# Reordering the stage between the layer-0 experts and the layer-1 attention

## The chip, the cores and the metric

The kernel runs on one core of one Trainium2 chip. The metric is the device time of one execution in microseconds (us). A profile of one execution, taken by the hardware profiler, is the source of every row below; its times count from the span's start.

## What is computed

Two layers over 512 latent tokens with a prefix of 256 context tokens, 1024 channels, in float32. Layer 0 mixes tokens by pooling, layer 1 by grouped-query attention; each layer ends in 16 experts of which a token uses two. Each sub-layer normalises its input and modulates it with vectors that come from a conditioning vector through `w_mod`:

```python
def modulate(x, g, shift, scale):
    return rmsnorm(x, g) * (1.0 + scale) + shift
...
    qkv = h_lat @ w_qkv
    q = rmsnorm(qkv[..., :Q_DIM].reshape(B, S, N_Q_HEADS, HEAD_DIM), q_g)
    k = rmsnorm(qkv[..., Q_DIM:Q_DIM + KV_DIM].reshape(B, S, N_KV_HEADS, HEAD_DIM), k_g)
    v = qkv[..., Q_DIM + KV_DIM:].reshape(B, S, N_KV_HEADS, HEAD_DIM)
...
    x = x + g1 * y_lat
    x = x + g2 * hier_moe(modulate(x, norm2_g[i], sh2, sc2), ...)
```

The shift of layer 1's first sub-layer is made of chunks 0 and 1 of `w_mod`, its scale of chunks 2 and 3. Latent and context tokens have vectors of their own.

## The kernel before

Tokens are cut into six tiles of 128 rows (two of context, four latent). All instructions stand in an order written by hand; each engine runs its own in that order and waits on semaphores for the others.

**Weights.** The list `order` (lines 267 to 280) fixes the order of all weight loads. Each load is 1 MB, 2048 words in each of 128 partitions. `fill` (line 282) issues the next ones on SP's queue for as long as a place is free and the list has not come to `state["until"]`; `done` gives a place back and fills again, `cap(n)` sets how many of the main places may be filled. Main place i begins at word 48416 - 2048(i + 1): place 0 at 46368, 1 at 44320, 2 at 42272, 3 at 40224, 4 at 38176. Two further places lie in the middle region (`mid`), and two extra ones at words 33728 and 29376, which are used from the middle of attention until the experts of layer 1 (`state["extra"]`, set in `between`). A place is free when no tile lies in it. Tiles come from the class `Arena`: `take` gives the first room that fits, from word 22528 up for plain float32 tiles. A load is issued in the program's order, so one that waits for its place holds up all that SP issues after it.

**Splits.** Products for which float32 is asked for are made of three matmuls on a high and a low part (`mm3`, lines 478 to 481). `split` (lines 473 to 476) makes the parts: ScalarE casts, VectorE or GpSimd subtracts. `split_w` (line 1091) does it for a quarter of a block of `w_qkv`; block 4 holds the keys, block 5 the values, blocks 0 to 3 the queries. The parts of two blocks fit into `w8`, four expert unit buffers of 2048 words.

**Modulation rows.** `mod_row` (line 409) multiplies the conditioning vectors with a chunk of `w_mod` in two halves of eight matmuls (line 415) and splits the result (lines 422, 424). `mod_spread` (line 426) spreads a row over all partitions by a matmul (line 437) and copies it out; for a scale chunk it also multiplies with the norm's gain (lines 434, 442).

**The stage of the change.** The experts of layer 0 call hooks: after expert 13 row 0 is made, after expert 14 row 1, and at the end `last` (line 1117) runs: cap 3, spreads of chunks 0 and 1, splits of the keys, row 2, splits of the values, row 3, spreads of chunks 2 and 3, a square root of a single column, a change of the middle region, and two more unit buffers. Then comes the loop for further blocks (line 874), for experts with more tokens than a tile holds. It uses the last four unit buffers and the count `nb` of blocks; in the profiled execution it has no iteration. Behind it SP loads row tiles 0 to 3 from `accD` (line 1149), into which the experts' results are added by scattering DMAs on GpSimd's queue (line 792). A tile is squared and its root taken on ScalarE (`norm`, lines 457 and 1208), then scaled and shifted on VectorE (`prep`, lines 1214 to 1216), transposed and split (`turn_rows`), and projected on the key and the value weights, twice 24 matmuls. From line 1242 on: norm and prep of tile 0, a fill for the query weights, norm and prep of tile 1, turn_rows of tile 0, norm of tile 2, the load of tile 4, then the loop over six tiles.

**What follows.** The query stage uses four scratch tiles of 2048 words, attention four tiles P of 768 words, four PT of 1536 and the vectors of layer 1. In attention `between` gives the scratch tiles back one by one, lifts the cap to 2, 3 and 4, opens the two extra places, and then works through chunks 4 to 9 of `w_mod`. At the end of attention (from line 1425) the tiles go, the cap is 3, ScalarE's queue loads the four residual row tiles from `accD` (line 1442), the rest of `wo` is split, and `gated` (lines 1453, 1454) adds the first half of the attention's output to the residual before the last two splits.

Of the kernel before, what the change touches and what calls it, by code (L numbers as in the profile page):

```python
# [14 lines left out]
AF = mybir.ActivationFunctionType  # L15
# [5 lines left out]
D = 1024  # L21
S = 512
L = 256
NT = 6
# [4 lines left out]
NE = 16  # L29
# [10 lines left out]

BEFORE = 6
BESIDE = (4, 6)
CAPS = dict(pool=6, moe0=(7,) * 11 + (5,), qkv=3, query=2, attend=(2, 2, 3, 4), wo=3, moe1=(7, 7, 6, 5))


def band_table():
# [179 lines left out]
def backbone(ctx: ExitStack, tc: tile.TileContext, a: dict, out: bass.AP):  # L226
    nc = tc.nc
    V, A, G, T = nc.vector, nc.scalar, nc.gpsimd, nc.tensor
# [15 lines left out]
    def stream_mod(l, chunks):  # L244
        for c in chunks:
            for h in range(2):
                order.append((("mod", l, c, h), a["w_mod"][l, c, h], (4, 512)))
# [5 lines left out]
    def stream_experts(l, between={}):  # L253

        for e in range(-2, NE):
            if e + 2 < NE:
                for h in range(2):
                    order.append((("wgu", l, e + 2, h), a["moe_wgu"][l, nth(e + 2), h], (4, 2 * FE)))
            if e >= 0:
                order.append((("wd", l, e), a["moe_wd"][l, nth(e)], (2, D)))  # L260
            for m, c in between.get(e, ()):
                stream_mod(m, [c])

    def stream_qkv(c):
        order.append((("qkv", c), a["attn_wqkv"][c], (8, 256)))
# [2 lines left out]
    order.append((("pool",), a["pool_w"], (8, 256)))  # L268
    stream_mod(0, range(6, 10))
    stream_experts(0, {-2: [(0, 10), (0, 11)], 12: [(1, 0)], 13: [(1, 1)]})  # L270
    stream_qkv(4)
    stream_qkv(5)
    stream_mod(1, range(2, 4))
    for c in range(4):
        stream_qkv(c)
    stream_mod(1, range(4, 10))
# [641 lines left out]
    m0 = Moe(0, NT)  # L918
# [172 lines left out]
    def split_w(c, q, eng=V):  # L1091

        i = (4 * c + q) % 8
        u = shaped(w8[:, 1024 * i:1024 * i + 1024], [128, 2, 2, 256])
        split(u[:, 0], u[:, 1], get("qkv", c)[:, 2 * q:2 * q + 2, :], eng)
        if q == 3:
            done("qkv", c)
        return u
# [4 lines left out]
    wkv = {}  # L1103

    def mod1_row(*chunks):
        for c in chunks:
            for _ in mod_row(1, c, mod1[c]):
                pass
# [3 lines left out]
    def spread1(*chunks):  # L1112
        for c in chunks:
            for _ in mod_spread(sm, 1, c // 2, c % 2, mod1[c], {v: bc["BA"[c // 2], v] for v in range(2)}):
                pass

    def last():

        state["until"] = ("qkv", 0)
        cap(CAPS["qkv"])  # L1120
        pb.split(t=(2, 1), y=(2, 1), m=(4, 1))
        bc.update({(n, v): sx.tile([128, D]) for n in ("B", "A") for v in range(2)})
        spread1(0, 1)
        wkv[4] = [split_w(4, q) for q in range(4)]
        mod1_row(2)
        wkv[5] = [split_w(5, q) for q in range(4)]
        mod1_row(3)
        spread1(2, 3)

        A.activation(m0.sb.tile([128, 1]), eps, AF.Sqrt)  # L1130
        pb.split(t=(2, 1), u=(2, 1), y=(2, 1), i=(1, 1), m=(1, 1))
        ar.swap("mid")
        for _ in range(2):
            m0.more_units()

    m0.experts(accD, CAPS["moe0"], more, {
        11: tables, 12: lambda: state.update(mid=0), 13: lambda: mod1_row(0), 14: lambda: mod1_row(1), NE: last})
    m0.sb.free()
    m0.mb.free()


    ab = ar.scope()
    vv = ab.tile([128, NT, 256])
    xb = [sx.tile([128, D]) for t in range(4)]
    x = [xb[t % 4] for t in range(NT)]
    sx.reserve(2, [128, D], "h1")

    def load_rows(t):
# [48 lines left out]
        V.tensor_sub(c[:, :, 1, :], q, c[:, :, 0, :])  # L1197

    sk = ar.scope()
    wK, wV = wkv[4], wkv[5]  # L1200
    r = sk.tile([128, NT])
    ks = sk.tile([128, NT, 4])
    pb.split(t=(4, 1), k=(2, 1), v=(2, 1))
# [1 line left out]
    def norm(t):  # L1205
        if t < NT:
            square_sum(sk, x[t], r[:, t:t + 1])
            A.activation(r[:, t:t + 1], r[:, t:t + 1], AF.Sqrt, scale=1.0 / D, bias=eps)

    def prep(t):  # L1210
        if t < NT:
            v = 1 if t < 2 else 0
            h1[t] = sx.tile([128, D], name="h1", bufs=2)
            V.tensor_mul(h1[t], x[t], bc["A", v])
            V.reciprocal(r[:, t:t + 1], r[:, t:t + 1])
            V.scalar_tensor_tensor(h1[t], h1[t], r[:, t:t + 1], bc["B", v], op0=OP.mult, op1=OP.add)  # L1216
# [18 lines left out]
    def store_key(t):  # L1235
        for kv in range(0, 4, 2):
# [2 lines left out]
                T.transpose(p2[:, j, :], kc[t][:, kv + j // 2, j % 2].rearrange("p a d -> p (a d)"), ident)  # L1239
            A.copy(kT[:, kv:kv + 2, :, t * 128:t * 128 + 128], p2.rearrange("p (a b) c -> p a b c", a=2))  # L1240

    norm(0)
    prep(0)
    state["until"] = None
    fill()
    norm(1)
    prep(1)
    turn_rows(0)
    norm(2)
    load_rows(4)  # L1250
    for t in range(NT):
        PK[t] = pb.get("k", [128, 256])
        project(PK[t], t, wK)
        if t:
            key(t - 1)
            A.copy(vv[:, t - 1, :], PV[t - 1])
        if t + 1 < NT:
            turn_rows(t + 1)
            if t + 5 < NT:
                load_rows(t + 5)  # L1260
        square_heads(sk, PK[t], ks[:, t, :])
        A.activation(ks[:, t, :], ks[:, t, :], AF.Sqrt, scale=1.0 / HEAD, bias=eps)
        norm(t + 3)
        prep(t + 2)
        PV[t] = pb.get("v", [128, 256])
        project(PV[t], t, wV)
        if t:
            store_key(t - 1)
    wq = {0: [split_w(0, q) for q in range(4)]}
# [272 lines left out]
```

## Time and profile before

| what | us |
|---|---|
| three runs | 931.96, 924.33, 931.01 |
| their median | 931.01 |
| the profiled execution | 926.72 |
| its span, first to last instruction | 924.9 |

In the rows PE is TensorE (PEld its weight loads), DVE VectorE, ACT ScalarE, POOL GpSimd, SP the engine that issues most loads; ACTq and SPq are their queues. L415 is line 415. A timeline row gives the start, the time, the engine, line and operation, output and input tile, their shape and the count; in brackets stands how long the engine had been idle and what ended it. PEclk is TensorE's granted clock, 1.00 for 2.4 GHz and 0.50 for 1.2 GHz.

### The profile page before, as it was taken

The numbers are of one execution on the slowest core, as the hardware profiler recorded it, in microseconds if no ns is written. First come the engines' busy times: TensorE is split into PE (matmuls) and PEld (weight loads), VectorE is DVE, ScalarE is ACT, GpSimd is POOL, SyncE is SP. The second block draws the span as 40 slices with busy tenths as digits, with TensorE's granted clock in tenths as the row PEclk, the third lists the DMA queues.
The fourth block names the chain that finished last, engine by engine and source line by source line (L and its number), as shares of the span: only waits on it lengthen the run. The fifth ranks groups of instructions, "written<-read, shape, count | busy, mean of one in ns | idle before, by whom it ended". The sixth has DMA issues, their size and how long they took to land. (4 is left out here: it accounts for less than half of the span.)

```text
span 924.9 us, 12774 instructions
## 1 busy us (share of the span) xinstructions
PE 802.5 (87%) x4593; PEld 541.8 (59%) x4593; DVE 614.0 (66%) x1077; ACT 481.9 (52%) x1006; POOL 172.8 (19%) x164
## 2 busy tenths in 40 slices
PE   4699958989999865998879999999979599999994
PEld 0256735567766514987766566566657355666551
DVE  3552778799998545746666677768245678888761
ACT  2534346446555335755568677679323364555440
POOL 1052332223333210003200000002200212332211
PEclk9899977999999975999999999999998789999997
DMA  8997369989998966011101332310074599999961
GB/s 339 418 349 311 128 217 413 348 300 357 377 362 304 356 217 273 2 47 46 46 1 46 139 135 92 109 74 27 20 311 196 203 364 309 343 335 330 344 239 29
DMA packets 36722, 204.80 MB, mean 221 GB/s; under 512 B 6660, under 2 KB 6740, under 8 KB 16816
## 3 DMA queue, kind: packets, MB, share of 16 engines
q1 hardware_dynamic: 24976, 172.06, 48.5%
q0 software_dynamic: 10032, 27.30, 11.3%
q10 hardware_dynamic: 1648, 4.60, 1.3%
q8 instruction: 37, 0.61, 0.3%
q14 instruction: 29, 0.24, 0.1%
HBM read 187.15 MB, written 25.17 MB: 230 GB/s over the span
## 5 line engine op out<-in xcount | busy, mean ns | idle before, releaser
L479 PE MATMUL banks<-low 128*128 128x512 f32 (+2 forms) x404 | 154.6, 383 | 6.1 <-DVE main L1191 4.4
L480 PE MATMUL banks<-low 128*128 128x512 f32 (+2 forms) x404 | 150.3, 372 | 7.4 <-DVE low L476 7.4
L481 PE MATMUL banks<-low 128*128 128x512 f32 (+2 forms) x404 | 150.3, 372 | 0.0
L476 DVE TENSOR_TENSOR low<-main,low 128x1024 fp32r<-128x1024 f32 (+1 forms) x121 | 129.8, 1129 | 22.4 <-ACT low L475 22.0
L475 ACT CAST low<-main 128x1024 fp32r<-128x1024 f32 (+1 forms) x137 | 119.3, 933 | 5.9 <-DMA main<-in_moe_wgu_dram 2.8
L1380 DVE TENSOR_REDUCE main<-banks 128x1 f32<-128x768 f32 x64 | 61.1, 955 | 43.7 <-PE banks L1376 43.3
L479 PEld LDWEIGHTS banks<-low 128*128 128x128 f32 (+1 forms) x404 | 74.6, 185 | 24.4 <-ACT low L475 6.9
L480 PEld LDWEIGHTS banks<-low 128*128 128x128 f32 (+1 forms) x404 | 74.6, 185 | 22.4 <-DVE low L476 8.0
L481 PEld LDWEIGHTS banks<-low 128*128 128x128 f32 (+1 forms) x404 | 74.5, 184 | 17.3 <-DVE low L476 0.8
L790 PE MATMUL banks<-main 128*128 128x512 f32 (+1 forms) x176 | 81.1, 604 | 2.4 <-SPq L874 1.5
L415 PE MATMUL banks<-main,cT 128*32 128x512 f32 x376 | 61.4, 756 | 14.3 <-DMA main<-in_w_mod_dram 12.4
L476 POOL TENSOR_TENSOR low<-main,low 128x512 fp32r<-128x512 f32 x16 | 20.7, 1296 | 282.2 <-ACT low L475 282.2
L1398 ACT COPY main<-banks 128x384 f32<-128x384 f32 x128 | 56.0, 487 | 33.5 <-PE banks L1397 33.1
L1401 ACT ACTIVATE main<-banks,main 128x768 f32<-128x768 f32 x64 | 63.7, 996 | 8.4 <-DVE main L1384 3.5
L742 POOL DMA_INDIRECT main<-hD,main x32 | 42.1, 1317 | 118.5 <-issue 39.6
L776 ACT COPY main<-banks 128x256 f32<-128x256 f32 (+1 forms) x32 | 11.1, 346 | 100.2 <-PE banks L774 92.7
L791 DVE TENSOR_TENSOR main<-banks,main 128x512 f32<-128x512 f32 (+1 forms) x64 | 43.0, 687 | 30.5 <-PE banks L790 28.9
L470 PE MATMUL banks<-ident,main 128*128 128x128 f32 (+2 forms) x384 | 49.7, 273 | 13.8 <-DVE main L1216 9.3
L1397 PE MATMUL banks<-ident,main 128*128 128x128 f32 x384 | 54.1, 274 | 4.3 <-ACT mid L1285 2.0
L1409 PE MATMUL banks<-main 128*64 128x256 f32 x384 | 53.8, 394 | 2.0 <-DVE low L1387 2.0
L470 PEld LDWEIGHTS banks<-ident,main 128*128 128x128 f32 (+2 forms) x384 | 42.0, 145 | 20.5 <-DVE main L1216 10.0
L790 PEld LDWEIGHTS banks<-main 128*128 128x128 f32 (+1 forms) x176 | 30.4, 181 | 37.5 <-issue 32.3
(258 smaller groups left out, 1471.5 us busy)
## 6 DMA issues: line engine op xcount, KB each, us to landing
main<-in_moe_wgu_dram SPq DMA_DIRECT2D x50, 1024.0 KB
main<-in_w_mod_dram SPq DMA_DIRECT2D x47, 1024.0 KB
main<-in_moe_wd_dram SPq DMA_DIRECT2D x22, 1024.0 KB
mid<-in_moe_wgu_dram SPq DMA_DIRECT2D x14, 1024.0 KB
mid<-in_moe_wd_dram SPq DMA_DIRECT2D x10, 1024.0 KB
main<-in_attn_wqkv_dram SPq DMA_DIRECT2D x6, 1024.0 KB
hD<-main POOLq DMA_DIRECT2D x9, 512.0 KB, 3.3
main<-in_attn_wo_dram SPq DMA_DIRECT2D x4, 1024.0 KB
```

Of the source, the lines that this page charges most:

```text
L415: T.matmul(p[32 * j:32 * j + 32, :], cT[:, 4 * h + j, :], w[:, j, :], start=h == 0, stop=h == 1)
L470: T.transpose(p[:, k, :], src[:, c * 128:c * 128 + 128], ident[:n, :n])
L475: A.copy(hi, src)
L476: eng.tensor_sub(lo, src, hi.bitcast(F32))
L479: T.matmul(p, xh, wh, start=first, stop=False)
L480: T.matmul(p, xh, wl, start=False, stop=False)
L481: T.matmul(p, xl, wh, start=False, stop=last)
L790: T.matmul(p, hT[:, k, :], wd[:, k, cols], start=k == 0, stop=k == 1)
L1380: V.reduce_max(m[:, 0:1], p, axis=AX.X)
L1397: T.transpose(p2[:, j, :], Ps[u][:, k * 128:k * 128 + 128], ident)
L1398: A.copy(PT[u // 4, hh][:, 3 * g3:3 * g3 + 3, 128 * q2:128 * q2 + 128], p2)
L1401: A.activation(Ps[step], p, AF.Exp, bias=mx[step][:, 0:1], scale=rq, accum_out=mx[step][:, 1:2])
```

## The change

Chunks 2 and 3 of layer 1's `w_mod` are loaded ahead of the key and value weights. The hook at the end of the experts makes row 2, spreads chunks 0 and 1, makes row 3, spreads chunks 2 and 3, and splits the keys, all ahead of the loop; the cap of the stage is 2. The stop at the first query block is set from expert 13 on. The two further unit buffers go, and the middle region changes behind the loop. The value weights are split behind prep of tile 1. The single square root stands behind the loop. turn_rows of tile 0 comes ahead of norm and prep of tile 1, and the fill for the query weights behind the value splits. Two tiles, `gap`, of 1024 words are taken and never used.

```diff
@@ -40,7 +40,7 @@
 
 BEFORE = 6
 BESIDE = (4, 6)
-CAPS = dict(pool=6, moe0=(7,) * 11 + (5,), qkv=3, query=2, attend=(2, 2, 3, 4), wo=3, moe1=(7, 7, 6, 5))
+CAPS = dict(pool=6, moe0=(7,) * 11 + (5,), qkv=2, query=2, attend=(2, 2, 3, 4), wo=3, moe1=(7, 7, 6, 5))
 
 
 def band_table():
@@ -268,9 +268,9 @@
     order.append((("pool",), a["pool_w"], (8, 256)))
     stream_mod(0, range(6, 10))
     stream_experts(0, {-2: [(0, 10), (0, 11)], 12: [(1, 0)], 13: [(1, 1)]})
+    stream_mod(1, range(2, 4))
     stream_qkv(4)
     stream_qkv(5)
-    stream_mod(1, range(2, 4))
     for c in range(4):
         stream_qkv(c)
     stream_mod(1, range(4, 10))
@@ -1114,35 +1114,34 @@
             for _ in mod_spread(sm, 1, c // 2, c % 2, mod1[c], {v: bc["BA"[c // 2], v] for v in range(2)}):
                 pass
 
+    def hold():
+        mod1_row(0)
+        state["until"] = ("qkv", 0)
+
     def last():
 
-        state["until"] = ("qkv", 0)
         cap(CAPS["qkv"])
         pb.split(t=(2, 1), y=(2, 1), m=(4, 1))
         bc.update({(n, v): sx.tile([128, D]) for n in ("B", "A") for v in range(2)})
+        mod1_row(2)
         spread1(0, 1)
-        wkv[4] = [split_w(4, q) for q in range(4)]
-        mod1_row(2)
-        wkv[5] = [split_w(5, q) for q in range(4)]
         mod1_row(3)
         spread1(2, 3)
-
-        A.activation(m0.sb.tile([128, 1]), eps, AF.Sqrt)
+        wkv[4] = [split_w(4, q) for q in range(4)]
         pb.split(t=(2, 1), u=(2, 1), y=(2, 1), i=(1, 1), m=(1, 1))
-        ar.swap("mid")
-        for _ in range(2):
-            m0.more_units()
 
     m0.experts(accD, CAPS["moe0"], more, {
-        11: tables, 12: lambda: state.update(mid=0), 13: lambda: mod1_row(0), 14: lambda: mod1_row(1), NE: last})
+        11: tables, 12: lambda: state.update(mid=0), 13: hold, 14: lambda: mod1_row(1), NE: last})
     m0.sb.free()
     m0.mb.free()
+    ar.swap("mid")
 
 
     ab = ar.scope()
     vv = ab.tile([128, NT, 256])
     xb = [sx.tile([128, D]) for t in range(4)]
     x = [xb[t % 4] for t in range(NT)]
+    gap = [sx.tile([128, D]) for t in range(2)]
     sx.reserve(2, [128, D], "h1")
 
     def load_rows(t):
@@ -1197,7 +1196,6 @@
         V.tensor_sub(c[:, :, 1, :], q, c[:, :, 0, :])
 
     sk = ar.scope()
-    wK, wV = wkv[4], wkv[5]
     r = sk.tile([128, NT])
     ks = sk.tile([128, NT, 4])
     pb.split(t=(4, 1), k=(2, 1), v=(2, 1))
@@ -1239,18 +1237,21 @@
                 T.transpose(p2[:, j, :], kc[t][:, kv + j // 2, j % 2].rearrange("p a d -> p (a d)"), ident)
             A.copy(kT[:, kv:kv + 2, :, t * 128:t * 128 + 128], p2.rearrange("p (a b) c -> p a b c", a=2))
 
+
+    A.activation(r[:, NT - 1:NT], eps, AF.Sqrt)
     norm(0)
     prep(0)
+    turn_rows(0)
+    norm(1)
+    prep(1)
+    wkv[5] = [split_w(5, q) for q in range(4)]
     state["until"] = None
     fill()
-    norm(1)
-    prep(1)
-    turn_rows(0)
     norm(2)
     load_rows(4)
     for t in range(NT):
         PK[t] = pb.get("k", [128, 256])
-        project(PK[t], t, wK)
+        project(PK[t], t, wkv[4])
         if t:
             key(t - 1)
             A.copy(vv[:, t - 1, :], PV[t - 1])
@@ -1263,7 +1264,7 @@
         norm(t + 3)
         prep(t + 2)
         PV[t] = pb.get("v", [128, 256])
-        project(PV[t], t, wV)
+        project(PV[t], t, wkv[5])
         if t:
             store_key(t - 1)
     wq = {0: [split_w(0, q) for q in range(4)]}
```

## Rows read from the trace of the kernel before

**Rows 1.** The page: busy time, then tenths in 40 slices of the span.

```profile
PE 802.5 (87%) x4593; PEld 541.8 (59%) x4593; DVE 614.0 (66%) x1077; ACT 481.9 (52%) x1006; POOL 172.8 (19%) x164
...
DMA  8997369989998966011101332310074599999961
```

**Rows 2.** Timeline of TensorE, 330 to 363: start us, us, engine, line.

```profile
331.30 1.07 PE L415 MATMUL banks<-main,cT 128*32 128x512 f32 x8
...
335.47 1.93 PE L415 MATMUL banks<-main,cT 128*32 128x512 f32 x8 [3.10 <-DMA main<-in_w_mod_dram]
...
340.53 1.94 PE L415 MATMUL banks<-main,cT 128*32 128x512 f32 x8 [2.40 <-DMA main<-in_w_mod_dram]
...
343.85 1.93 PE L415 MATMUL banks<-main,cT 128*32 128x512 f32 x8 [1.39 <-DMA main<-in_w_mod_dram]
...
359.21 1.97 PE L470 MATMUL banks<-ident,main 128*128 128x128 f32 x8 [9.26 <-DVE main L1216]
...
362.34 0.58 PE L481 MATMUL banks<-low,mid 128*128 128x256 f32 x1 [0.54 <-DVE mid L476]
```

**Rows 3.** Windows from 330 on: length, busy us (instructions), PEclk, DMA share, GB/s.

```profile
340.00:345.00 5.00, 3.09 (x16) 0.43 (x16) 1.94 (x4) 0.82 (x2) 0.00 (x0) 0.50 0.27 98
...
360.00:365.00 5.00, 4.46 (x20) 3.94 (x19) 2.85 (x5) 2.51 (x5) 0.00 (x0) 0.50 1.01 424
...
375.00:380.00 5.00, 5.00 (x45) 5.00 (x44) 4.25 (x9) 4.44 (x15) 0.00 (x0) 1.00 0.01 2
```

**Rows 4.** End of attention: timeline of SP, ScalarE, VectorE, TensorE; one of the waits.

```profile
674.92 0.80 SPq L295 DMA_DIRECT2D main<-in_moe_wgu_dram  x2
...
674.94 1.97 ACTq L1442 DMA_DIRECT2D main<-accD  x4
...
DVE main L1454 <- DMA main<-accD: 6.2, 3, 2.3
...
693.83 1.29 DVE L476 TENSOR_TENSOR low<-main,low 128x512 fp32r<-128x512 f32 x2
...
694.57 0.80 PE L480 MATMUL banks<-low 128*128 128x512 f32 x1 [7.04 <-DVE low L476]
...
696.54 0.77 PE L479 MATMUL banks<-low 128*128 128x512 f32 x1
...
700.54 0.40 PE L480 MATMUL banks<-low 128*128 128x512 f32 x1
```

**Rows 5.** Timeline of SP's DMA issues, 312 to 353; us ends with the last.

```profile
312.45 1.57 SPq L295 DMA_DIRECT2D main<-in_attn_wqkv_dram  x2
...
315.77 20.14 SPq L295 DMA_DIRECT2D main<-in_w_mod_dram  x4
...
325.27 4.71 SPq L295 DMA_DIRECT2D main<-in_w_mod_dram  x2
...
351.61 1.77 SPq L1149 DMA_DIRECT2D main<-accD  x4
```

**Rows 6.** Timeline of ScalarE and VectorE, 332 to 377.

```profile
332.38 2.19 ACT L475 CAST low<-main 128x512 fp32r<-128x512 f32 x4
...
333.05 2.50 DVE L476 TENSOR_TENSOR low<-main,low 128x512 fp32r<-128x512 f32 x4 [2.70 <-ACT low L475]
...
354.88 1.06 ACT L457 ACTIVATE main<-main 128x1024 bf16<-128x1024 f32 x1 [0.89 <-DMA main<-accD]
...
356.05 1.28 ACT L1208 ACT_TABLE_LOAD   x1
...
357.35 0.29 ACT L1208 ACTIVATE main<-main,eps 128x1 f32<-128x1 f32 x1
...
376.29 1.04 ACT L457 ACTIVATE main<-main 128x1024 bf16<-128x1024 f32 x1
```

**Rows 7.** Waits of SP, 330 to 362: us in total, times, longest us.

```profile
SPq L874 <- DVEq L873: 7.4, 1, 7.4
SPq L874 <- DMA accD<-main: 5.4, 2, 4.9
```


## The prediction

> **What bounds the kernel now.** I read the page's busy table and slices first: TensorE is busy 87% of the span and the DMA engines are full in both expert stages but nearly empty in the attention between them [rows 1]. So a change can only pay where TensorE stands still, and there are two such places that the change can reach. The windows and the timeline show the first: after the experts of layer 0 TensorE waits for the modulation rows (chunk 2's second half starts at 335.47, chunk 3's halves at 340.53 and 343.85, each after a wait for in_w_mod), then from about 350 until 359.21 it does nothing, 9.26 us, waiting for VectorE's first normalised tile [rows 2]. In that time the DMA engines run dry: share 0.27 in 340:345 [rows 3]. TensorE comes back at 0.50 of its clock (1.2 GHz) and runs 20 matmuls in 4.46 us where it later, at 1.00, runs 45 in 5.00 [rows 3]. The second place is the end of attention: TensorE waits 7.04 us at 694.57 for a split that VectorE makes late, because VectorE waited 6.2 us for the residual rows out of accD [rows 4]. Those rows were asked for at 674.94, the same moment at which SP asks for the first two expert weights of layer 1 [rows 4].
>
> **Part 1: the order of the six loads.** At one freed place each, SP issues now: key and value weights at 312.45 and 313.70, chunk 2's halves at 315.77 and 325.27, chunk 3's at 329.66 and 335.58 [rows 5]. The last waits for the key splits, whose first pass ends at 333.05 + 2.50 = 335.55 [rows 6]. Putting chunks 2 and 3 in front leaves the moments that places come free as they are, so the loads by name become: chunk 2 at 312.45 and 313.70, chunk 3 at 315.77 and 325.27, key weights at 329.66. With the cap at 2 the value weights take place 0, which chunk 2's first half leaves about 330.1 (its eight matmuls can start when the last down projection ends near 329.6, and take 1.07 us, the row at 331.30 [rows 2]). I give each load the landing of the load that has its issue time now: the first three are in by 331.30, the fourth at 335.47, the fifth at 340.53 [rows 2]. Value weights, 5.5 us earlier than the sixth load now, land by 343.85 at the latest.
> From chunk 3's second half to SP's release take now 351.61 - 343.85 = 7.76 us [rows 2, 5]; from 335.47 that gives 343.2. The key splits now come behind the spreads and ahead of the loop: 3.17 us from first cast to last subtraction (332.38 to 335.55 [rows 6]), so 340.53 + 3.17 = 343.70, and SP issues some 0.4 later, 344.1. A third arrival is the scatter of the last expert: SP's two long waits at the loop are 4.9 us for accD and then 7.4 us for VectorE, the latter ending just before 351.61 [rows 7], so the scatters land at about 344.0. All three agree; I take 344.4 for the row loads against 351.61: **7.2 us**. Bounds: the value load now competes with the last scatter, and 1 MB at 424 GB/s [rows 3] is 2.5 us, so 4.7 at worst; 8.4 if only the spreads hold SP (343.2).
>
> **Part 2: the loop and the square-root table.** The loop for further blocks now uses the last four of six unit buffers; two of them lie under the value splits, which is why these go behind the loop. The loop runs no iteration here, so the buffers cost nothing, and moving the change of the middle region behind it costs at most a wait for weights read long ago: 0. The warm-up activation ahead of the loop goes, and one comes behind it. In the trace the first one is in vain: the square at 354.88 is followed by a table load of 1.28 us at 356.05 before the root at 357.35 [rows 6], on the chain to the first tile. With a root issued behind the loop, its load lies in the 3.27 us from 351.61 to 354.88 in which the rows travel [rows 5, 6]; no square after 357.35 reloads. Saved: **1.3 us**; bounds 0 (the square still wants its own set) and 1.3.
> The Trainium skill, ScalarE: Activation LUTs, What ACT_TABLE_LOAD costs, puts a switch of set at some 1.28 us of load and 1.38 us of drain, 2.66 in all. The row has 0.02 us between the load's end and the root, so I see no drain; by the page the saving would be 2.7 and the time 1.4 us less.
>
> **Part 3: order of tiles and value splits.** turn_rows(0) moves ahead of the second tile's norm. Today VectorE finishes prep(1) before the first subtraction, and the third matmul of the projection waits 0.54 us [rows 2]; now the subtraction is next in line: **0.5 us**. The value splits, 2.50 us of VectorE like the key's [rows 6], stand behind prep(1). By the offsets of the trace the first tile's product ends at 350.6, subtractions 353.9, prep(1) 356.5, value splits 359.0. TensorE's first projection of 24 matmuls at half clock (4.46/20 each [rows 3]) lasts until about 357.3, eight transposes go to 358.1, and the first value projection needs the third quarter of the splits (358.4) only at its 13th matmul: hidden. If that cover is gone, the cost is at most the 2.5 us.
> A wait is added on SP: the fill for the query weights wants place 0, held until the value splits end at 359.0; behind it stand the second query block and row tiles 4 and 5. Two blocks and a half-megabyte tile at 424 GB/s, 2 us after issue, bring tile 4 at about 367. Its square is at 376.29 now [rows 6], about 367.2 then; ScalarE may wait a fraction of a us, and TensorE needs that tile only three projections later: 0, at worst 1. Two places instead of three mean that query blocks 2 and 3 are asked for when blocks 0 and 1 are split, four projections of 24 x 0.111 us = 10.7 us [rows 3] ahead of use, with the queue idle: 0.
> First place in all: 7.2 + 1.3 + 0.5 = **9.0 us**.
>
> **Part 4: where the tiles come to lie.** The two gap tiles hold no data. They push the two h1 tiles from 29312 to 31360 and the small key tiles behind 33408. When the query stage asks for room, first fit then gives its scratch 2 the words 29376 to 31424 (now it misses by 64 words, since the key tiles begin at 31360, and goes to 33728) and scratch 3 goes to 33728 instead of 35776. In attention the four P tiles then lie at 22824 and 31424 to 33728 (now 22824 and 29376 to 31680) and the PT tiles at 35776 to 41920 (now up to 42432). So place 2 (42272 to 44320) and the extra place at 29376, both covered now, are free: five places in attention instead of three. The stream then runs two loads further: the last modulation half leaves a place for the first expert load, and the first wo block for the second, all in a stage with idle queues [rows 1]. At 674.9 nothing is left for SP to issue until the next wo block is split at about 678. The residual rows, four of 0.5 MB, have the queues alone: 2.1 MB at 424 GB/s [rows 3] are 5 us, and with one modulation load beside the tail they are in by 685, while VectorE adds the fourth at 687. Its 6.2 us of waits go. The split that TensorE waits for comes at 688.3 instead of 694.5; TensorE then stands 0.7 us, and 0.5 more for the first product's transposes, not 7.04. It also keeps its clock: from 696.54 to 700.54 it runs 11 steps of 512 columns in 4.00 us [rows 4]; at 1.00 a 256-column one takes 5.00/45 = 0.111 us [rows 3], so I estimate 0.22 for these, 2.4 us in all, and with the same ratio on the two steps and the transposes from 694.57 to 696.54 some 2.3 us come back. Sum 7.04 - 1.2 + 2.3 = **8.1 us**. Bounds: 0 if the places do not come free, 9.3 if TensorE does not stand at all. In the expert stage of layer 1 TensorE is dense and the bytes still to load are the same, so the gain is carried to the end.
>
> **Sum.** 926.72 (span 924.9 and 1.8 around it) - 9.0 - 8.1 = 909.6. The profiled execution is 4.3 us below the median of the runs, 931.01, so the forecast for a median is 931.0 - 17.1 = **914**.
>
> **Rivals.** (a) Only the first place gains: something I have not placed still covers place 2 or 29376, or the rows come late for another reason. 931.0 - 9.0 = 922. For it: the argument is by words of memory, no row shows it. Against: both extra addresses fit the scratch tiles exactly. (b) Only the second gains, because the scatters or the value load hold the loop until 351 anyway: 931.0 - 8.1 = 923. For it: the accD wait ends only near 344, and the value load is 1 MB more in the queue; against: the DMA share is already down at 0.27 in 340:345 now [rows 3]. (c) The change does not do what it says, both at nothing: 931. (d) Slower: TensorE's clock does not come back in the key and value stage, because value splits on ScalarE and VectorE open gaps between its matmuls. The stage has 12 projections of 24 matmuls; at 0.50 a matmul costs 0.223 instead of 0.111 us [rows 3]. Now some 20 run slow [rows 3]; beyond about 150 more slow ones (17.1/0.112) the gain is used up, and with all 268 the loss is 30.0 and the time 944. Against: the clock rises now in spite of the 0.54 us gap, and my offsets leave no larger one.
>
> **How the numbers follow.** About 1%, 9.3 us, is what a measurement of this kernel can tell from no change (three runs lie 7.6 apart). Forecast 0.68, with its own range 907 to 920; (a) 0.14; (b) 0.08; (c) 0.05; (d) 0.05. Faster by over 1% (under 921.7): nearly all of the forecast and half of (a) and (b), which sit on the bound: 0.75. Slower: (d) and a little of the rest, 0.07. Same: 0.18. The range 903 to 926 takes in the forecast, (a) and (b).
>
> **What would show it.** Right: row loads by SP at 344 to 345; no table load between the first square and its root; TensorE's first transposes at about 350.7 (359.21 now); two layer-1 expert loads issued before the end of attention; no wait for accD at the residual add, and TensorE's 7 us gap under 2. Wrong: the accD or in-flight wait at the loop ending after 348; a first value projection with gaps; expert loads still issued with the residual rows.

## The result and the profile after

The changed kernel took 914.93 us (median of four runs, 913.24 to 916.75), the kernel before 929.53 beside it: ratio 0.9863, 95% interval 0.9824 to 0.9902, so 12.7 us saved, between 9.1 and 16.4. This ratio, like all that follow, is an estimate with its interval and not the quotient of the two medians, which lie 14.6 apart. Forecast was 914.0, a gain of 17.1. The profiled execution took 913.42 with a span of 911.6.

From the page of the changed kernel [rows 1]:

```profile
PE 800.0 (88%) x4593; PEld 540.1 (59%) x4593; DVE 613.8 (67%) x1077; ACT 479.4 (53%) x1004; POOL 173.1 (19%) x164
...
DMA  8979268989999993311210542220155699999962
```

The work is the same (TensorE has as many instructions, VectorE too, ScalarE two fewer). What went is idle time. Two loads have moved forward in the DMA row: slices 27 and 29 read 2 and 1 where they read 1 and 0, and slice 30, in which attention ends, reads 5 where it read 7 (the slices of the two pages do not cover quite the same stage).

TensorE behind layer 0's experts [rows 2], start, length, engine, line, and in brackets the idle time with what ended it:

```profile
339.47 1.06 PE L415 MATMUL banks<-main,cT 128*32 128x512 f32 x8 [0.61 <-DMA main<-in_w_mod_dram]
...
354.63 1.97 PE L470 MATMUL banks<-ident,main 128*128 128x128 f32 x8 [11.05 <-DVE main L1214]
...
357.14 0.58 PE L481 MATMUL banks<-low,mid 128*128 128x256 f32 x1
```

Here a shift has to be taken out first. Layer 0's last down product ends at 329.62 in the trace of before and at 333.63 in this one. The 4.01 us arise almost wholly in the first 105 us, in code that is the same in both. So from here on times of the first place are counted from that end, called zero. The transposes come 21.00 us behind zero, against 29.59. The wait of 0.54 at the third matmul of the projection is gone.

SP's issues in the timeline [rows 5], the second fence its waits at the loop [rows 7] (us in total, times, longest):

```profile
333.66 1.35 SPq L295 DMA_DIRECT2D main<-in_attn_wqkv_dram  x2
348.35 1.77 SPq L1148 DMA_DIRECT2D main<-accD  x4
```

```profile
SPq L874 <- DMA accD<-main: 10.0, 2, 5.0
...
SPq L874 <- DMA main<-in_attn_wqkv_dram: 0.5, 1, 0.5
SPq L874 <- DVEq L873: 0.4, 1, 0.4
```

The row loads leave 14.72 behind zero; predicted was 344.4, which is 14.8 behind. The last three waits follow one another: the puts (the scattering DMAs into `accD`), VectorE at the last of the key splits (0.4 more), the value weights (0.5 more). VectorE's timeline ahead of the loop:

```profile
344.29 1.29 DVE L442 SCALAR_TENSOR_TENSOR main<-banks,main 128x512 f32<-128x512 f32 x2 [0.73 <-ACT main L434]
345.50 2.49 DVE L476 TENSOR_TENSOR low<-main,low 128x512 fp32r<-128x512 f32 x4
```

The last spreads (line 442) and then the key splits (line 476) follow one another without a gap, and the splits end at 347.99, 0.36 ahead of the row loads. VectorE held SP for 7.4 before.

ScalarE's timeline on the way to the first tile [rows 6]:

```profile
348.35 1.28 ACT L1241 ACT_TABLE_LOAD   x1 [1.71 <-DVEq L874]
349.65 0.20 ACT L1241 ACTIVATE main<-eps 128x1 f32<-128x1 f32 x1
351.58 1.06 ACT L457 ACTIVATE main<-main 128x1024 bf16<-128x1024 f32 x1 [1.73 <-DMA main<-accD]
...
352.76 0.29 ACT L1206 ACTIVATE main<-main,eps 128x1 f32<-128x1 f32 x1
```

The table is loaded while the rows travel; between square and root nothing is left.

The end of attention in the timeline [rows 4], SP, ScalarE's queue and TensorE:

```profile
596.12 44.51 SPq L295 DMA_DIRECT2D main<-in_moe_wgu_dram  x2
...
670.76 1.79 ACTq L1443 DMA_DIRECT2D main<-accD  x4
...
684.10 0.50 PE L480 MATMUL banks<-low 128*128 128x512 f32 x1 [0.75 <-DVE low L476]
...
685.30 0.65 PE L470 MATMUL banks<-ident,main 128*128 128x128 f32 x4 [0.47 <-DVE main L522]
...
688.11 0.39 PE L480 MATMUL banks<-low 128*128 128x512 f32 x1
```

Layer 1's first two expert loads leave SP at 596.12 and 640.30, long before the residual rows at 670.76. VectorE no longer waits for accD there, and TensorE's stop of 7.04 is 0.75 and 0.47. From the last output cast of attention (ScalarE, 0.06 before the rows are asked for) to the first routing matmul it takes 46.95 instead of 55.68, and to the end of the span 240.90 instead of 250.02.

### The profile page after: what moved, and what is told of

It reads as the page before. It is cut to its first block, busy times and chain, and to the rows that moved or that the text cites. A ratio compares the mean times of both kernels' runs of the same rounds, so it can differ in the third digit from the quotient of the medians.

```text
span 911.6 us, 12768 instructions
## 1 busy us (share of the span) xinstructions
PE 800.0 (88%) x4593; PEld 540.1 (59%) x4593; DVE 613.8 (67%) x1077; ACT 479.4 (53%) x1004; POOL 173.1 (19%) x164
## 5 line engine op out<-in xcount | busy, mean ns | idle before, releaser
L479 PE MATMUL banks<-low 128*128 128x512 f32 (+2 forms) x404 | 153.0, 379 | 5.9 <-DVE main L1190 4.4
L480 PE MATMUL banks<-low 128*128 128x512 f32 (+2 forms) x404 | 148.2, 367 | 1.1 <-DVE low L476 1.1
L481 PE MATMUL banks<-low 128*128 128x512 f32 (+2 forms) x404 | 148.5, 368 | 0.0
L479 PEld LDWEIGHTS banks<-low 128*128 128x128 f32 (+1 forms) x404 | 73.2, 181 | 23.9 <-ACT low L475 6.7
L481 PEld LDWEIGHTS banks<-low 128*128 128x128 f32 (+1 forms) x404 | 72.9, 180 | 17.1 <-DVE low L476 0.8
L480 PEld LDWEIGHTS banks<-low 128*128 128x128 f32 (+1 forms) x404 | 73.3, 182 | 15.9 <-DVE low L476 1.7
L470 PEld LDWEIGHTS banks<-ident,main 128*128 128x128 f32 (+2 forms) x384 | 41.8, 145 | 22.2 <-DVE main L1214 11.4
```

Of the source, the lines that this page charges most:

```text
L470: T.transpose(p[:, k, :], src[:, c * 128:c * 128 + 128], ident[:n, :n])
L479: T.matmul(p, xh, wh, start=first, stop=False)
L480: T.matmul(p, xh, wl, start=False, stop=False)
L481: T.matmul(p, xl, wh, start=False, stop=last)
```

## The experiments

The table has each profiled execution's stages: from zero to the row loads, to the first transposes and to the last output cast, then from that cast to the routing matmul and to the end of the span. The kernels are those of the experiments below; each row is one execution.

| kernel | rows | transposes | cast | to routing | to end |
|---|---|---|---|---|---|
| before | 21.99 | 29.59 | 345.26 | 55.68 | 250.02 |
| changed | 14.72 | 21.00 | 337.07 | 46.95 | 240.90 |
| no gap tiles | 14.99 | 21.34 | 337.33 | 55.73 | 249.26 |
| gap tiles alone | 21.96 | 29.64 | 345.36 | 47.10 | 244.81 |
| hold by order | 18.00 | 24.37 | 338.87 | 46.96 | 239.71 |
| values ahead | 19.09 | 25.50 | 341.52 | 46.94 | 240.28 |
| order alone | 18.43 | 26.10 | 341.24 | 55.85 | 249.00 |
| root in the chain | 15.91 | 23.56 | 338.18 | 46.97 | 239.67 |
| keys behind | 12.45 | 19.23 | 333.85 | 46.94 | 241.25 |
| loads behind the cast | 14.11 | 20.42 | 334.60 | 51.43 | 245.82 |
| keys halved | 12.78 | 19.09 | 333.66 | 47.12 | 240.33 |
| loads with the rows | 13.91 | 20.17 | 334.83 | 55.88 | 247.86 |
| turn behind | 17.31 | 23.59 | 340.46 | 47.41 | 239.60 |
| changed, again | 15.02 | 21.38 | 335.76 | 46.99 | 240.16 |

**The two places apart.** First the changed kernel without the gap tiles, then the kernel before with nothing but them.

```diff
-    gap = [sx.tile([128, D]) for t in range(2)]
```

> The changed kernel without the two gap tiles. By the theory of places, the words 29376 to 31424 and place 2 are covered again in attention, so the two expert loads are issued at the end of attention with the residual rows, TensorE's stall there is 7 us again, and the stage from the cast of the last attention output to the end of the span lasts 250 us (as before), not 241. The stage from the end of the last down product to the first transposes stays at 21.0 us. Time 8 to 9 us above the changed kernel, 923. Rival (the end of attention gained by its phase or clock, not by places): no difference, 915.

> The kernel before with the two gap tiles added and nothing else. By the theory of places: two expert loads are issued before the end of attention, the stall falls from 7.0 to 0.7 us, the stage from the cast of the last attention output to the end of the span lasts 241 us, the stage ahead of the first transposes stays at 29.6 us; 921 against 929.5. Rival: no difference.

Without the gap tiles: 917.94, ratio 0.9898 (0.9862 to 0.9934), 9.5 us saved. With them alone: 920.92, ratio 0.9931 (0.9904 to 0.9958), 6.4 saved. The sum is 15.9, and the table shows that each part moves its own stage and leaves the other as it was. The time without the gap tiles is better than the 923 that was expected: the last stage loses its 8.4 us as forecast (249.26 against 240.90), but the time is 3.0 above the changed kernel's 914.93 and 5.8 above the 912.19 of the next kernel, which is the changed one in effect. Without the gap tiles VectorE waits for the rows again (a row of its waits), and TensorE stands as before at the end of attention (its timeline):

```profile
DVE main L1454 <- DMA main<-accD: 6.2, 3, 2.3
```

```profile
686.43 0.80 PE L480 MATMUL banks<-low 128*128 128x512 f32 x1 [6.95 <-DVE low L476]
```

With them alone the stop is 0.91 (TensorE's timeline) and routing comes 8.6 us sooner behind the cast:

```profile
687.65 0.50 PE L480 MATMUL banks<-low 128*128 128x512 f32 x1 [0.91 <-DVE low L476]
```

But 3.8 of it are lost between routing and the end (197.71 us against the changed kernel's 193.95), where TensorE has a wait that it has not in the changed kernel. From its timeline:

```profile
751.20 1.51 PE L470 MATMUL banks<-ident,main 96*128 96x96 f32 x8 [3.21 <-DMA main<-hD,main]
```

Whether that kernel always has it stays open. What both runs show is that rivals (a) and (b), one part without the other, each fell.

**Holding the expert loads back, first try.** The changed kernel, with the queue's list stopped ahead of layer 1's experts until attention is over.

```diff
         state["extra"] = 2
+        state["until"] = ("wgu", 1, 0, 0)
         fill()
...
+    state["until"] = None
     cap(CAPS["wo"])
```

> The changed kernel, places free as they are, but the stream stops ahead of the first expert load until the end of attention, as it does in the kernel before for want of places. If it is the two expert loads beside the residual rows that cost the time (contention in the DMA queues), the 7 us stall and the half clock behind it come back and the time is 8 us above the changed kernel, 923. Rival (the earlier modulation loads, or other data in other words, bring the gain): 915.

The edit did nothing to the times of issue. It only moved the issues down in the program, and SP, which has nothing else to do there, ran ahead to them (its timeline):

```profile
594.96 42.97 SPq L295 DMA_DIRECT2D main<-in_moe_wgu_dram  x2
```

Neither theory is tested by it. It is the changed kernel a second time: 912.19, ratio 0.9837 (0.979 to 0.9884), 15.1 us saved. But its row loads leave at 18.00 behind zero, not 14.72, and this is of use. SP waits 4.0 for VectorE at the loop, and the cause lies further back, in the landing of chunk 3's second half (TensorE's timeline):

```profile
337.86 1.11 PE L415 MATMUL banks<-main,cT 128*32 128x512 f32 x8 [3.50 <-DMA main<-in_w_mod_dram]
```

That is 8.74 behind zero (329.12) where the changed kernel has 5.84 (339.47 - 333.63). From there to the row loads it is 9.26 here and 8.88 there, the spreads and the key splits. Why that half lands later stays open.

**The value splits ahead of the loop.**

```diff
         wkv[4] = [split_w(4, q) for q in range(4)]
+        wkv[5] = [split_w(5, q) for q in range(4)]
...
-    wkv[5] = [split_w(5, q) for q in range(4)]
```

(With the region change and two buffers as the kernel before has them there.)

> The changed kernel with the value splits ahead of the loop again, and with the two further unit buffers that they then need. If putting them behind the loop matters, SP is released only when the value load has landed (14.1 us behind the last down product in the changed kernel) and its splits are done, 3.2 us later: row loads at 17.7 instead of 14.7 us, first transposes at 24 instead of 21.0; 918. Rival (the order of the loads is all): 21, 915.

TensorE's timeline, then VectorE's:

```profile
337.59 1.07 PE L415 MATMUL banks<-main,cT 128*32 128x512 f32 x8 [2.46 <-DMA main<-in_w_mod_dram]
```

```profile
343.73 4.90 DVE L476 TENSOR_TENSOR low<-main,low 128x512 fp32r<-128x512 f32 x8
```

Eight subtractions instead of four. From the modulation half's matmuls to the row loads it is 11.4 us (348.99 - 337.59), 2.1 more than the 9.26 above. So putting the value splits behind the loop is worth some 2 us, where 3 was expected. The time, 913.76 (ratio 0.9856, 0.9806 to 0.9907), does not resolve that.

**The order alone.** The kernel before, with the modulation halves first in the list and the spreads ahead of both splits.

```diff
+    stream_mod(1, range(2, 4))
     stream_qkv(4)
     stream_qkv(5)
-    stream_mod(1, range(2, 4))
...
+        spread1(0, 1)
...
         spread1(2, 3)
+        wkv[4] = [split_w(4, q) for q in range(4)]
+        wkv[5] = [split_w(5, q) for q in range(4)]
```

> The kernel before with only the load order (all four row halves ahead of the key and value weights) and the order of rows, spreads and splits changed; both splits stay ahead of the loop, the places stay as they were. Counted from the end of layer 0's last down product. Theory (the modulation rows' last load ends last ahead of the loop): spreads end some 12 us in when that load is in time, 8 vector subtractions of both splits (4.9) follow, row loads 17 to 19 us in against 22.0 before, first transposes 24 to 26 in against 29.6, the end of attention as before (TensorE stall near 7, routing matmul 55.7 behind the last cast): 3 to 5 us faster, 923 to 925. Rival (the loop's entry hangs on the last put or the value weights, and the order gives nothing): row loads 21 to 22 in, 928.

925.59, ratio 0.9982 (0.996 to 1.0004): 1.7 us, and hardly to be told from nothing. In the stages it is 3.5 to the transposes and 4.0 to the cast, as expected. Chunk 3's half lands 7.03 behind zero, and the row loads leave 11.4 later, as with the values ahead. The order moves the modulation rows out of the chain, but both splits take their place: by itself it is worth half of the 8.2 that the changed kernel gains up to the cast.

**The root.** The changed kernel without the lone root behind the loop.

```diff
-    A.activation(r[:, NT - 1:NT], eps, AF.Sqrt)
```

> The changed kernel without the lone square root behind the loop, so that the table is loaded at the first norm's root. Theory: the load (1.28) stands between the first square and its root, first transposes 7.6 us behind the row loads' issue instead of 6.3, and 1.3 us more in all, not readable in one time. Rival (the table load lies beside the vector product, and the chain does not lengthen): 6.3 and no change.

ScalarE's timeline:

```profile
348.48 1.06 ACT L457 ACTIVATE main<-main 128x1024 bf16<-128x1024 f32 x1 [5.04 <-DMA main<-accD]
...
349.64 1.28 ACT L1206 ACT_TABLE_LOAD   x1
350.94 0.29 ACT L1206 ACTIVATE main<-main,eps 128x1 f32<-128x1 f32 x1
```

From row loads to transposes 7.65 us, against 6.28 and 6.36 in the two profiles of the changed kernel, and 7.60 before. The load's 1.28 is all that is added there. The one time, 908.90, says nothing about so small a piece.

**The key splits behind the loop.** SP's waits say that they end last, so they were moved into the time in which the rows travel, and the value weights held behind the row loads.

```diff
-        state["until"] = ("qkv", 0)
+        state["until"] = ("qkv", 5)
...
-        wkv[4] = [split_w(4, q) for q in range(4)]
...
     for t in range(4):
         load_rows(t)
+    state["until"] = ("qkv", 0)
+    fill()
+    wkv[4] = [split_w(4, q) for q in range(4)]
```

> The changed kernel with the key splits moved directly behind the loop (they lie in the wait for the rows) and the value weights' load held until the row loads are issued. Theory (three arrivals end the wait at the loop, the key splits the last of them by a little, more when the last modulation load is late): the wait now ends with the last put, some 13.6 us behind the last down product, or with the spreads, 12 to 15 in; row loads 14 us in when the modulation load is in time and up to 16 when late, against 14.7 and 18.0 to 19; first transposes 6.3 to 6.6 behind them; 0.5 to 2.4 us faster than the changed kernel: 911.5 to 913.5, ratio to before near 0.983. Rival (the value weights' transfer beside the rows delays the second rows, or the splits hold the first square and the first projection): 1 to 2 us slower, 915 to 917.

The one wait that SP has left at the loop, and VectorE and ScalarE in the timeline:

```profile
SPq L874 <- DMA accD<-main: 9.3, 2, 6.2
```

```profile
342.57 1.23 DVE L1214 TENSOR_TENSOR main<-main 128x1024 f32<-128x1024 f32 x1
...
343.10 1.04 ACT L457 ACTIVATE main<-main 128x1024 bf16<-128x1024 f32 x1
```

Only the puts are left to wait for, and the row loads leave 12.45 behind zero (14 was expected, with the puts ending the wait later). Half a us of it goes again, because ScalarE, with four casts and the table load, starts the square 0.53 late. 910.37, ratio 0.9832 (0.9796 to 0.9869), with runs from 903.78 to 915.38. Two of the four quarters were then moved on, behind the first norm:

> The changed kernel with the value weights' load held until the row loads are issued, and of the key splits two quarters directly behind the loop and two behind the first block's norm. Theory (with all four behind the loop ScalarE's first square started at 343.10 although the rows were there at 342.57; two casts less, 1.1, let it start with the rows): row loads 12.5 to 15 us behind the last down product, first transposes 6.3 behind them instead of 6.8, 0.5 us under the kernel with all four there; some 910, ratio to before near 0.982. Rival (the two late quarters hold the first projection): a wait of 1 or more at the first projection's matmuls, no gain over the changed kernel, 914.

ScalarE and VectorE in the timeline:

```profile
347.85 1.06 ACT L457 ACTIVATE main<-main 128x1024 bf16<-128x1024 f32 x1 [0.46 <-DMA main<-accD]
...
347.85 1.23 DVE L1214 TENSOR_TENSOR main<-main 128x1024 f32<-128x1024 f32 x1 [0.92 <-DMA main<-accD]
```

Square and product now start together when the rows land, and the transposes come 6.31 behind the row loads. No matmul of the first projection waits. 908.21, ratio 0.9801 (0.9765 to 0.9837), the lowest median of the study; the changed kernel beside it had 910.71 and 0.9834 (0.9799 to 0.987). The intervals overlap: the gain is seen in the stages of these single executions (2.3 us to the transposes, with chunk 3's half at 6.00 and 5.91 behind zero), not in the time.

**Holding the expert loads back, second try.** This time the first load waits for an instruction: for the last output cast, or for the product ahead of it (there `late` is the matmul that fills `po`).

```diff
         state["extra"] = 2
+        state["until"] = ("wgu", 1, 0, 0)
         fill()
...
-            A.copy(os[0][:, done_c, :], po[done_c])
+            late = A.copy(os[0][:, done_c, :], po[done_c])
...
+    state["until"], state["after"] = None, late.ins.name
     cap(CAPS["wo"])
```

> The changed kernel with the places unchanged, but layer 1's expert loads made to wait for the last output cast of attention. Theory (what the places gave is the expert loads' early issue, which keeps them out of the residual rows' way): expert loads within 1 us behind the last cast, a wait of some 6 for the residual rows, TensorE stall near 7, routing matmul 55 to 56 behind the last cast, the end 249 behind it: the changed kernel's time plus 8, some 922. Rival (the gain at the end of attention comes from something else that the places changed): stall under 1, routing at 47, 914.

> As the kernel whose expert loads wait for the last output cast, but they wait for the product ahead of that cast, so that they are issued beside the first residual row load and not 0.55 us behind it. Theory (which transfer is issued first decides): waits of some 6 in all for the residual rows, TensorE stall near 7, routing matmul 55 to 56 behind the last cast, the end 249 behind it. Rival (the other half of the gain has another cause in the places): stall 3.4, routing 51.4, end 245.8, as with the wait for the cast.

The first, with the loads 0.55 us behind the first row load (669.79 against 669.24), gave half of the loss at the end of attention (51.43 to routing); its one time is 916.79. VectorE's wait for the rows and TensorE's timeline:

```profile
DVE main L1457 <- DMA main<-accD: 2.7, 2, 2.3
```

```profile
685.20 0.50 PE L480 MATMUL banks<-low 128*128 128x512 f32 x1 [3.37 <-DVE low L476]
```

The second, with both at the same moment, gave all of it (55.88; its one time is 919.13), with the places of memory as the changed kernel has them. The same two rows:

```profile
DVE main L1457 <- DMA main<-accD: 6.6, 3, 2.3
```

```profile
689.40 0.80 PE L480 MATMUL banks<-low 128*128 128x512 f32 x1 [7.31 <-DVE low L476]
```

So the places matter because they let the loads go early; nothing else about them is needed for the 8.7 us to routing.

**The order of the tiles.** The changed kernel with the first tile's transposes behind the second's norm, as before.

```diff
     prep(0)
-    turn_rows(0)
     norm(1)
     prep(1)
+    turn_rows(0)
```

> The changed kernel with the first block's transposes put behind the second block's norm, as in the kernel before. Theory: the transposes start when they did (TensorE waits for the first norm alone), their evictions stand on VectorE behind the second norm, and the first projection starts up to 3 us later; with the first norm at 21.0 us and the second rows' load close behind, 0.5 to 2 us lost in all. Rival (the order is without effect, since both norms are ready together): under 0.3.

TensorE's timeline:

```profile
357.13 1.97 PE L470 MATMUL banks<-ident,main 128*128 128x128 f32 x8 [10.26 <-DMA main<-accD]
...
360.26 0.58 PE L481 MATMUL banks<-low,mid 128*128 128x256 f32 x1 [0.54 <-DVE mid L476]
```

The old wait of 0.54 is back. From transposes to third matmul it is 3.13 us, against 2.51 in the changed kernel. That is the low end of what was expected. The one time, 915.37, says nothing about it, since the row loads of that execution are late (17.31).

**The changed kernel once more.**

> The changed kernel once more, to tell whether its gain is the 12.7 of its first comparison or the 17.1 of the sum. If the shortfall is the spread of single executions (the start of the program, the instants at which the clock falls), the stage times stay as they were (last cast 335 to 339 us behind layer 0's last down product, the end 240 to 241 behind the cast) and the time is 911 to 914, ratio 0.983 to 0.985. If the sum was too high by 4, the time is 914 to 916, ratio 0.986 to 0.988.

910.71 (906.33 to 918.67), ratio 0.9834, 15.4 us saved, between 12.1 and 18.7. The cast comes 335.76 behind zero and the end 240.16 behind the cast. The first theory holds as far as this reaches: the stages are as they were and the ratio lies where it said; the time is 0.3 under its 911.

## Why the prediction was right

**Part 1, 7.2 us.** The profiled execution gives the times of the text: chunk 3's second half at 339.47, which is 335.46 on the clock of the trace of before (335.47 in the text), the key weights' cast at 344.47, so 340.46 (340.53), the row loads at 344.34 (344.4). "Each load gets the landing of the load that has its issue time now" was the right rule. Two steps came out right by luck. The text counts the key splits from the landing of their weights (340.53 + 3.17); in the rows VectorE begins them behind the spreads, which in that execution end at nearly the same time. And it has the puts land at about 344.0 before, from the end of VectorE's wait; but between that end and the row loads SP has about 1 us more, 0.4 of it a further wait, so that they landed at about 343. Both matter, because the 7.2 hold for that execution. In the eight that have the same code up to the loop (the changed kernel twice, no gap tiles, hold by order, root, turn, both late loads) the row loads leave 13.9 to 18.0 behind zero, 15.5 in the mean. In each they follow chunk 3's second half by 8.9 to 9.4, the spreads and then the key splits, and that half starts between 5 and 9 behind zero. So the gain is 6.5 in the mean, 4.0 to 8.1 singly (the text's bounds were 4.7 and 8.4). "All three agree" was true of one landing; where the half is late, the other two arrivals hide nothing.

**Part 2, 1.3 us.** 7.60 from row loads to transposes became 6.28; undone, 7.65. Of the three table loads before (at 349.87, 352.71 and 356.05) one is left; only the last stood on the chain, as the text has it. The Trainium skill, ScalarE: Activation LUTs, What ACT_TABLE_LOAD costs, has 1.38 us of drain beside the load, which would have made it 2.7. In the rows the next activation starts 0.02 behind the load's end (349.65, 350.94), and undoing it cost 1.3 to 1.4: no run here shows the drain.

**Part 3, 0.5 us.** Undone, it cost 0.6 at the third matmul. The value splits are hidden, as forecast: no matmul of the first value projection waits. Tile 4's square waits 0.44 for its load (0 to 1 was forecast), and TensorE does not notice. The cap of two places was not undone by itself; in the stage that it bears on the two traces stay nearly as far apart as they were, 9.9 us at 375 us and 9.7 at 488 us, counted from zero, so it costs next to nothing there.

**Part 4, 8.1 us.** 8.73 to the routing matmul, and 8.6 by itself. The stop went from 7.04 to 0.75 + 0.47, just as the text has it (1.2), which is 5.8; 2.9 are left. Of these 2.4 lie in the matmuls behind the stop, where the clock no longer falls: from the restart to the same matmul it was 5.97 (694.57 to 700.54 [rows 4]) and is 4.01 (684.10 to 688.11), less the 0.47 already counted. The rest lies later. The text's 2.3 rests on a miscount: from 696.54 to 700.54 there are ten steps, not eleven, which makes the same estimate 2.7. The order of the transfers as the cause is shown by the two late loads.

**Sum.** From zero to the end of the span it was 595.28 and is 577.97, 578.58 and 575.92 in the three profiles that run the changed program: 16.7 to 19.4 less, around the 17.1. For the first place 9.0 was forecast. The same transposes of a later tile, before and in the changed kernel (TensorE's timelines):

```profile
380.59 1.04 PE L470 MATMUL banks<-ident,main 128*128 128x128 f32 x8
```

```profile
374.72 1.03 PE L470 MATMUL banks<-ident,main 128*128 128x128 f32 x8
```

From zero that is 50.97 and 41.09, 9.88 less: 8.6 at the first transposes, 0.6 at the third matmul, and 0.7 that the text does not have, because TensorE's clock comes back (0.50 to 1.00) behind nine matmuls of the first projection instead of 17. Of the 9.88 some 1.5 are lost again later in attention in that execution (see the last section), and 8.2 are left at the cast.

In whole times it is 12.7, 15.1 and 15.4, with intervals that reach from 9.1 to 19.5; the medians lie 14.6, 15.8 and 18.0 apart. The median to which the 17.1 was applied, 931.01 of three runs, was high: beside the experiments the kernel before had 927.0 to 929.5. So it is in part luck that 914.0 lies so near the 914.93: from the 929.53 measured beside it the forecast would have been 912.4. What lies between 15 and 17 stays open; the profile of before is one execution, 0.3 to 2.8 us under these medians.

Rival (d) fell, since the clock comes back so early. Two windows of the changed kernel from just behind the restart (PE busy with its matmuls first, the granted clock third from the right); where 20 matmuls ran at 0.50 before [rows 3], there are 28 (at 0.63 in the mean) and then 45 (at 1.00):

```profile
355.00:360.00 5.00, 5.00 (x28) 4.55 (x27) 3.41 (x5) 3.92 (x8) 0.00 (x0) 0.63 0.03 7
360.00:365.00 5.00, 5.00 (x45) 5.00 (x44) 5.00 (x8) 4.84 (x17) 0.00 (x0) 1.00 0.19 48
```

## What to carry to other kernels

Look at what else is asked for in the microsecond in which a late operand is asked for: freeing two buffers early was worth as much here as a rebuilt stage, only because it took two prefetches out of the way of four small reads. A prefetch on a queue that runs ahead can't be delayed by its place in the program; it goes when its buffer is free, or behind an instruction that it waits for. And moving the last arrival forward pays only up to the next one: the load order alone gave 4.0 us up to the last cast of attention, and 1.7 us in the time, hardly to be told from nothing, until the splits that took its place at the head of the chain were moved as well.

## What the hardware showed that was not expected

**Reads that shared the DMA engines with larger packets got a third of them.** Packets, MB and share of the 16 engines' time of SP's queue (q1, weight loads, the expert loads first) and ScalarE's (q10, residual rows). With both issued at the same moment, from 673.4 to 685.4:

```profile
q1 hardware_dynamic: 455, 3.33, 66.6%
q10 hardware_dynamic: 460, 1.69, 34.6%
```

As many packets of each, but those of the loads are twice as long (7.3 KB against 3.7, MB by packets), and the rows are a third of the bytes. The Trainium skill, DMA: Bandwidth & Descriptors, Queues, rings and completion order, says that an engine takes a packet from each queue in turn; these counts agree. The changed kernel's rows, alone from 670.7 to 676.7:

```profile
q10 hardware_dynamic: 467, 1.73, 78.0%
```

Nearly the same bytes in half the time. The head start was worth more than its length: with the loads 0.55 us later the rows moved 0.80 MB in their first 4 us, with the loads beside them 0.20.

**TensorE's clock fell behind a short wait in one execution, and not in the other.** At one step of attention TensorE waits 1.68 us for ScalarE in both profiles of the changed kernel. The timeline and a window of the first (the granted clock third from the right):

```profile
607.85 0.76 PE L437 MATMUL banks<-partB,col 128*128 128x512 f32 x1 [1.68 <-ACT main L434]
```

```profile
608.00:611.00 3.00, 3.00 (x11) 2.49 (x11) 1.03 (x2) 0.43 (x1) 0.00 (x0) 0.50 0.02 5
```

and of the second:

```profile
603.04 0.50 PE L437 MATMUL banks<-partB,col 128*128 128x512 f32 x1 [1.68 <-ACT main L434]
```

```profile
594.00:614.00 20.00, 17.98 (x141) 12.60 (x137) 14.50 (x31) 15.03 (x34) 0.00 (x0) 1.00 0.07 29
```

In the first the matmul takes 0.76 instead of 0.50 and the clock is at its lower level behind it (0.50, 1.2 GHz), which costs some 1.5 us against the trace of before; in the second it stays at 1.00 (2.4 GHz).

**How far one execution is from the next.** Zero lies between 326.90 and 334.61 in the fourteen profiles, behind code whose instructions are nearly the same in all; the matmuls of one modulation half start 5 to 9 us behind zero; and one fall of the clock adds 1.5. The six times of the changed kernel's second measurement span 12 us. So pieces under 2 us were read from stages, not from times.
